# The attention's last four gated rows by seven products in front of w_o

## The chip, the cores and the metric

The kernel runs on one core of a Trainium2 chip. The metric is the device time of one execution in microseconds (us); lower is better. Before the change it is 2486.24 us, the median of three runs (2486.18 to 2487.11). The five engines named below are TensorE (PE, matrix products), VectorE (DVE), ScalarE (ACT), GpSimd (POOL) and SyncE (SP, which here issues the loads of weights). Each works through its own instructions in order and waits on semaphores for the others.

## The reference, cut to what matters

Two layers, each with a half-step feed-forward block, a mixer and another half-step feed-forward block. 640 tokens (512 of a new stream, 8 x 16 of running ones) share the weights; the model width is 1024. The change is inside the mixer:

```python
z = h @ w_in                                  # conv B | C | V | q | k | v | gates
g_conv, g_attn = split(sigmoid(g + b_gate))   # 1024 columns each
y_conv, _ = short_conv(B, C, V)               # 512 columns
y_attn = band_attention(q, k, v)              # 512 columns
m = g_conv * (y_conv @ w_conv_out) + g_attn * (y_attn @ w_attn_out)
x = x + m @ w_o
```

## The kernel before

Activations lie transposed: 128 features on the partitions, 640 tokens (T) along the free axis, in two halves of 320 (HT; `t1` and `t2`). Every float32 product is made of three matmuls of rounded parts, hi x hi, hi x lo and lo x hi; the parts of each weight and each operand are made on the chip, hi by an ACT cast and lo by a DVE subtraction. A plain product (`product`, line 434) of an output block of 128 features with 512 input features takes 4 x 3 x 2 = 24 matmuls of 128x128 by 320 columns.

Where it can, the kernel uses a seven-product scheme of the Strassen-Winograd kind in place of eight block products. Its seven operands are named X11, X21, X22, XT5 (parts of the input as it is, or one difference) and XN6, XT7, XT4 (mixtures of the two token halves of an even and an odd feature block). The weights are mixed too: a unit of kind "mix" is two raw tiles ra and rb, from which `source` (line 295 by way of `add`) makes four slabs: slab 0 is ra; slab 1 is a sum s and a sum in rb; slab 2 is a half that POOL has summed by an accumulating DMA (`one`, lines 280 and 281) and the half "raw<-s" that DVE sums; slab 3 is the second half of rb. A "plain" unit is one raw tile of eight 128x128 blocks. `prep` issues ACT's casts (whi, line 363), `flush` DVE's subtractions (wlo, line 368); slabs are prepared two ahead, with three buffers of each of raw, whi and wlo.

The mixer's second half is `outputs` (from line 1485 on). It runs with a written-out order: PE, DVE and ACT execute their instructions in the order of the program. It uses these pieces:

- `gate_pair(m)`: two gate columns m and m + 1 by seven products of 12 matmuls. PE works through X11, X21, XN6, XT5, XT7, X22, XT4. X11, XN6, XT7 and XT4 accumulate in one bank (pa, shown as qa). Between them ACT copies pa away: c1 after X11 (line 1512), u2 after XN6 (line 1522); c5 is copied out of pc after XT5 (line 1524). Between c1 and u2 ACT also has `due()` (sigmoids and copies that were put off), the casts of slab 2, what the hook at[0] does, and the cast of slab 3. DVE's add raw<-s for slab 2 is issued in the `prep` behind c1.
- `out(m)`: a plain product py of one output block (line 434), multiplied by its gate (line 1562), and, for the attention, added to the convolution's mm (line 295).
- `rows(name, ms)`: four output blocks at once by seven (line 1633), 84 matmuls, with their gating on DVE (lines 1640 and 1642). Before, only the convolution's blocks 4 to 7 go this way. `moved(0)` and `moved(1)` copy their gated results from the gates' buffers to mm by ACT (line 1647), moved(0) inside `rows`, ahead of its last product, and moved(1) in the `due` of the next pair.
- `mixed`: the DVE mixtures and parts of one pair of feature blocks of the convolution's y (lines 1590 and 1581), spread over the hooks.
- `take(ya)`: the parts of the attention's y (lines 234 and 235), in pair 8.
- `give(ms)`: the parts of the final m, spread over the last pair and the two last products; then w_o's eight products po (line 434), each over k = 0 to 7 in order, with x += po (line 1430) and the next block's operands (`ex.final`) behind each.

The gates' tiles take four rotating buffers; the banks of py, po and of the rows' two pairs of products take two; the parts of m take the eight buffers of the mixer's input h, which the gate pairs read to the end.

## Time and profile before

| what | value |
|---|---|
| median of 3 runs | 2486.24 us |
| profiled execution, its own time | 2487.08 us |
| its span, first to last instruction | 2485.3 us |
| mean granted TensorE clock | 0.999 |
| the mixer's second half, layer 0 / layer 1, seen from pair 8 to the end of w_o | 698.7 to 833.5 / 1930.1 to 2064.8 us |
| HBM read and written over the span | 99 GB/s |

Times in the profile are us from the span's start unless marked ns. A line in order of time gives the start, the duration, the engine, the line of the program, the operation with its output and inputs, the shapes, how many were merged, and in brackets how long the engine had idled and what released it. A matmul's own duration (0.31 us) is longer than its place in the pipeline, so the distance of starts counts.

### The profile page before, as it was taken

Reading aid. Unit: us, or ns where it says so; the run is one execution under the profiler, and the core shown is the slowest. Engines: PE = TensorE matmul, PEld = TensorE weight load, DVE = VectorE, ACT = ScalarE, POOL = GpSimd, SP = SyncE. Lnnn points to the kernel's source line nnn. Section 1 sums busy time; section 2 is a strip of 40 time slices with the busy share of each in tenths; the row PEclk is TensorE's granted clock in tenths of the full one; section 3 lists DMA queues with packets and bytes.
Section 4 is the critical chain, followed back from the end, with each engine's and each line's share of the span. In section 5 each row is a group of like instructions: output and inputs, shape, how many; then the busy total and the mean of one; then the engine's idle time right before and its main releaser. Section 6 shows DMA issues by size and latency. Waiting matters only on the chain.

```text
span 2485.3 us, 43991 instructions
## 1 busy us (share of the span) xinstructions
PE 2471.0 (99%) x17288; PEld 2418.2 (97%) x17288; DVE 2158.3 (87%) x3587; ACT 1373.0 (55%) x2196; POOL 317.4 (13%) x479
## 2 busy tenths in 40 slices
PE   9999999999999999999999999999999999999999
PEld 8999999889999999999999999998999999999998
DVE  7999998888886899998799999988878769999997
ACT  6555556665554555555665555556645455555555
POOL 0111112211000001111001111121110000111111
PEclk9999999999999999999999999999999999999999
DMA  4443445335343334444334443453453333443444
GB/s 155 126 118 102 123 119 121 113 109 177 104 118 108 94 101 106 112 117 120 108 94 109 110 118 102 116 128 107 132 173 92 115 111 89 107 116 106 113 117 117
DMA packets 113072, 287.11 MB, mean 116 GB/s; under 512 B 12928, under 2 KB 52480, under 8 KB 112864
## 3 DMA queue, kind: packets, MB, share of 16 engines
q1 hardware_dynamic: 69552, 220.10, 28.0%
q0 software_dynamic: 42880, 63.94, 13.7%
q8 instruction: 135, 2.21, 0.4%
q14 instruction: 73, 0.60, 0.1%
q10 hardware_dynamic: 432, 0.25, 0.0%
HBM read 238.43 MB, written 7.94 MB: 99 GB/s over the span
## 4 chain that ended last, share of the span: by engine, by line
PE 92%; DVE 4%; ACT 2%; DMA 1%; issue 1%; SPq 0%; DVEq 0%; ACTq 0%; POOLq 0%
PE pab L458 12%; PE paa L458 11%; PE pcb L458 6%; PE daa L1143 6%; PE pca L458 5%; PE dab L1143 5%; PE po L434 5%; PE qa L458 4%; PE py L434 3%; PE pbb L458 3%; PE dca L1143 3%; PE pba L458 3%; PE dcb L1143 2%; PE ma_qk L458 2%; PE ma_cv L458 2%; PE pv L1770 2%
## 5 line engine op out<-in xcount | busy, mean ns | idle before, releaser
L363 ACT CAST whi<-raw 128x512 fp32r<-128x512 f32 (+1 forms) x573 | 500.4, 878 | 371.3 <-PE pbb L458 46.0
L368 DVE TENSOR_TENSOR wlo<-raw,whi 128x512 fp32r<-128x512 f32 (+1 forms) x573 | 574.4, 1005 | 135.9 <-ACT whi L363 132.1
L363 ACT CAST whi<-s 128x1024 fp32r<-128x1024 f32 (+1 forms) x160 | 151.6, 947 | 313.3 <-issue 111.4
L458 PE MATMUL pab<-xhib,whi 128*128 128x320 f32 x704 | 217.5, 309 | 0.0
L458 PE MATMUL pab<-xlob,whi 128*128 128x320 f32 x704 | 217.0, 308 | 0.0
L458 PE MATMUL pab<-xhib,wlo 128*128 128x320 f32 x704 | 217.0, 308 | 0.0
L458 PE MATMUL paa<-xhia,whi 128*128 128x320 f32 x640 | 197.7, 309 | 0.2 <-DVE ga L295 0.2
L458 PE MATMUL paa<-xhia,wlo 128*128 128x320 f32 x640 | 197.5, 309 | 0.0
L458 PE MATMUL paa<-xloa,whi 128*128 128x320 f32 x640 | 197.4, 308 | 0.0
L368 DVE TENSOR_TENSOR wlo<-s,whi 128x1024 fp32r<-128x1024 f32 (+1 forms) x160 | 174.8, 1092 | 4.6 <-ACT whi L363 4.6
L1165 POOL DMA_DIRECT2D x<-c_a x80 | 70.0, 1022 | 573.8 <-ACT ahia L1047 205.5
L1165 POOL DMA_DIRECT2D x<-c_b x72 | 62.8, 1002 | 583.6 <-ACT ahib L1047 205.8
L458 PEld LDWEIGHTS pab<-xhib,whi 128*128 128x128 f32 x704 | 132.1, 188 | 0.9 <-issue 0.9
L458 PEld LDWEIGHTS pab<-xlob,whi 128*128 128x128 f32 x704 | 132.2, 188 | 0.0
L458 PEld LDWEIGHTS pab<-xhib,wlo 128*128 128x128 f32 x704 | 132.1, 188 | 0.0
L458 PEld LDWEIGHTS paa<-xhia,whi 128*128 128x128 f32 x640 | 120.1, 188 | 1.1 <-DVE ga L295 0.5
L458 PEld LDWEIGHTS paa<-xloa,whi 128*128 128x128 f32 x640 | 120.1, 188 | 0.2 <-DVE xloa L702 0.2
L458 PEld LDWEIGHTS paa<-xhia,wlo 128*128 128x128 f32 x640 | 120.1, 188 | 0.2
L295 DVE TENSOR_TENSOR raw<-s,raw 128x512 f32<-128x512 f32 x160 | 109.1, 682 | 0.0
L458 PE MATMUL pcb<-xhib,wlo 128*128 128x320 f32 x352 | 108.7, 309 | 0.0
L458 PE MATMUL pcb<-xlob,whi 128*128 128x320 f32 x352 | 108.5, 308 | 0.0
L458 PE MATMUL pcb<-xhib,whi 128*128 128x320 f32 x352 | 108.5, 308 | 0.0
(840 smaller groups left out, 8150.4 us busy)
## 6 DMA issues: line engine op xcount, KB each, us to landing
raw<-in_wst SPq DMA_DIRECT2D x375, 512.0 KB, 3.6
x<-c_a POOLq DMA_DIRECT2D x80, 160.0 KB, 4.6
x<-c_b POOLq DMA_DIRECT2D x72, 160.0 KB, 3.6
lent<-in_wst POOLq DMA_DIRECT2D x36, 256.0 KB, 3.9
kc<-in_kcache SPq DMA_DIRECT2D x32, 256.0 KB, 5.2
vc<-in_vcache SPq DMA_DIRECT2D x16, 512.0 KB, 4.8
one<-in_wst POOLq DMA_DIRECT2D x28, 256.0 KB, 4.1
x<-u_a POOLq DMA_DIRECT2D x40, 160.0 KB, 4.1
```

The costliest lines, as they stand in the source:

```text
L295: DVE.tensor_tensor(out=out, in0=a, in1=b, op=op)
L363: ACT.copy(hi[:, d], src[:, c])
L368: DVE.tensor_tensor(out=lo, in0=src, in1=hi.bitcast(F32), op=ALU.subtract)
L434: PE.matmul(ps[:, a, :HT], w, x[a] if isinstance(x, tuple) else x[:, a * HT : (a + 1) * HT], start=first and j == 0 and not seeded, stop=l ...
L458: PE.matmul(ps, a, b, start=start and kp == 0 and j == 0, stop=stop and kp == NP - 1 and j == 2, skip_group_check=True)
L1143: PE.matmul(ps[u], w, y, start=start and i == 0 and j == 0, stop=i == 1 and j == 2, skip_group_check=True)
L1165: POOL.dma_start(x[ms[2 * u + r]][:, cols], z[:, u], accum_op=ALU.add)
L1770: PE.matmul(pv[t], xx[:, t * P : (t + 1) * P], w[:, kk * AW : (kk + 1) * AW], start=c == 0 and kk == 0 and j == 0, stop=c == KT // 2 - 1 a ...
```

## The change

The attention's blocks 4 to 7 leave `out` and go through `rows`, so that they need the mixtures of the attention's y as well. The order becomes: pair 8, py 8 and 9, pair 10, py 10 and 11, pair 12, pair 14, rows. The mixtures of both pairs of feature blocks are made in one instruction each: `mix(0)` to `mix(3)` on DVE behind py 8 and py 9, their hi parts (`high`) on ACT and lo parts (`rest`) on DVE in the hooks of pairs 10 and 12 and behind py 10. The operand tiles of the two pairs become one tile of two. moved(0) goes from the convolution's rows into the `due` of pair 8, moved(1) into its at[0], and the gates' buffers are taken behind that `due`. The parts of m are made in another order: m 0 and 2 in pair 14, 1 and 3 inside the rows, 4 to 7 behind them. w_o's two first products are interleaved: k = 0, 2, 1, 3 of both, then k = 4 to 7 of both.

```diff
     out += gates[:2] + [("co", m) for m in range(4)] + gates[2:4] + [("rows", ("co", (4, 5, 6, 7)))]
-    for i in range(4):
+    for i in range(2):
         out += [gates[4 + i], ("ao", 2 * i), ("ao", 2 * i + 1)]
+    out += gates[6:] + [("rows", ("ao", (4, 5, 6, 7)))]
     return out + [("o", m) for m in range(KT)]
...
             hold[0] = True
+            first = [acc(f"po{l}_{m}") for m in range(2)]
+            ws = [[tiles.take() for _ in mo] for _ in first]
+            for ks in ((0, 2, 1, 3), range(KT // 2, KT)):
+                for p, w in zip(first, ws):
+                    for k in ks:
+                        multiply(p, w[k], mo[k], k == 0, k == KT - 1)
             for m in range(KT):
-                po = acc(f"po{l}_{m}")
-                product(po, mo)
+                po = first[m] if m < 2 else acc(f"po{l}_{m}")
+                if m > 1:
+                    product(po, mo)
                 ex.weights(m)
...
-            u, g = gates[m], gates[m + 1] = tmp(f"g{n}"), tmp(f"g{n}_1")
             s0 = quiet()
             block(pa, s0, 0, X11, every, True, True)
             ACT.copy(c1, pa)
             due()
+            u, g = gates[m], gates[m + 1] = tmp(f"g{n}"), tmp(f"g{n}_1")
             prep(used[0] + 1)
...
+        def minus(out, a):
+            DVE.scalar_tensor_tensor(out=out, in0=a, scalar=-1.0, in1=out, op0=ALU.mult, op1=ALU.subtract)
...
+        za = yas.rearrange("p (i c) (a b) -> p i (c a) b", i=2, a=2)
+
+        def mix(n):
+
+            e1, e2, o1, o2 = (za[:, :, k] for k in range(4))
+            if n == 0:
+                add(e1, e1, e2, ALU.subtract)
+            elif n == 1:
+                add(e2, o2, e2, ALU.subtract)
+            else:
+                minus(*((o2, e1) if n == 2 else (o1, o2)))
+
+        def place(k):
+            if k == XT5:
+                return [(*(u[:, t2] for u in ya[2 * i]), za[:, i, 0]) for i in range(2)]
+            c = EXTRA.index(k)
+            return [(*(u[:, :, c] for u in x["ao"]), za[:, :, 1 + c])]
+
+        def high(*ks):
+            for k in ks:
+                for hi, _, z in place(k):
+                    ACT.copy(hi, z)
+
+        def rest(*ks):
+            for k in ks:
+                for hi, lo, z in place(k):
+                    low(lo, z, hi)
...
             gated(0, [s1[:, u] for u in range(2)], t1)
+            if mid:
+                mid()
             mul(c, w, 1, XT5, True)
...
             gated(0, [s2[:, u] for u in range(2)], t2)
-            if then:
-                then()
-            if name == "co":
-                moved(0)
             mul(a, w, 0, XT4, False)
-            flush()
+            if not end:
+                flush()
             gated(1, a, t1, -1.0)
             if name == "co":
-                lates.append(lambda: moved(1))
+                lates.append(lambda: moved(0))
+                moves.append(lambda: moved(1))
+            if end:
+                flush()
...
+        def begun(*ms):
+            for m in ms:
+                mo[m] = tuple(hp.tile([P, T], F32R, tag=f"h{i}", name=f"m{l}_{m}{i}") for i in ("hi", "lo"))
+
+        def given(*ms):
+            for m in ms:
+                split(*mo[m], mm[m])
...
-        rows("co", (4, 5, 6, 7), yc)
-        for m in range(KT, 2 * KT, 2):
-            last = m == 2 * KT - 2
-            gate_pair(m, [none, none, (lambda: take(ya, "ya", range(CT), yas_)) if m == KT else
-                          (lambda: give(range(1))) if last else none])
-            out(m, ya, (lambda: give(range(1, 4))) if last else None)
-            out(m + 1, ya, (lambda: give(range(4, 6))) if last else None)
-        give(range(6, KT))
+        rows("co", (4, 5, 6, 7), None)
+        gate_pair(8, [lambda: moves[0](), none, lambda: take(ya, "ya", range(CT), srcs)])
+        room("ao")
+        out(8, ya, None, lambda: (mix(0), mix(1)))
+        out(9, ya, None, lambda: (mix(2), mix(3)))
+        gate_pair(10, [lambda: high(XN6), lambda: (rest(XN6), high(XT7)), lambda: (rest(XT7), high(XT4))])
+        out(10, ya, None, lambda: rest(XT4))
+        out(11, ya)
+        gate_pair(12, [lambda: high(XT5), lambda: rest(XT5), none])
+        gate_pair(14, [none, lambda: (begun(*range(4)), given(0, 2)), none])
+        rows("ao", (4, 5, 6, 7), None, lambda: given(1, 3), None, True)
+        begun(*range(4, KT))
+        total(4, 5)
+        given(4)
+        total(6, 7)
+        given(5, 6, 7)
         return mo
```

The host lays out the weight stream by the same order (`mixer_order`): four plain slabs of w_attn_out become two plain ones and a unit of kind mix, so that the number of raw tiles stays the same. `total(ms)` adds the gated rows to mm (before, `out` did so for all eight blocks), and `room("ao")` takes the shared tile of the mixtures' parts.

More of the change, by code (lines that the diff above doesn't have):

```diff
@@ L1566, in out @@
                 post()
-        yc, ya, mo = [], [], []
-        more = []
-        yas_ = [yas[:, c, :] for c in range(CT)]
+        yc, ya = [], []
+        mo = [None] * KT
+        srcs = [yas[:, c, :] for c in range(CT)]
+        x, moves = {}, []
         def take(y, name, cs, srcs):
@@ L1574, in take, with take_even, room, mixed @@
                 y.append(parts(gp, f"y{c}", f"{name}{l}_{c}", srcs[c]))
-        def give(ms):
-            for m in ms:
-                mo.append(parts(hp, "h", f"m{l}_{m}", mm[m]))
+        def take_even(c):
+            y = tuple(gp.tile([P, T], F32R, tag=f"y{c}{i}", name=f"ya{l}_{c}{i}") for i in ("hi", "lo"))
+            split(*(z[:, t1] for z in y), srcs[c][:, t1])
+            ya.append(y)
         def low(lo, z, hi):
             DVE.tensor_tensor(out=lo, in0=z, in1=hi.bitcast(F32), op=ALU.subtract)
-        def mixed(i, y, z):
-            z = z.rearrange("p c (a b) -> p (c a) b", a=2)
-            e1, e2, o1, o2 = (z[:, i] for i in range(4))
+        def room(name):
+            x[name] = tuple(gp.tile([P, 2, 3, HT], F32R, tag=f"x{i}", name=f"x{i}{name}{l}") for i in ("hi", "lo"))
+        def minus(out, a):
+            DVE.scalar_tensor_tensor(out=out, in0=a, scalar=-1.0, in1=out, op0=ALU.mult, op1=ALU.subtract)
+        def mixed(i):
+            z = ycp[i].rearrange("p c (a b) -> p (c a) b", a=2)
+            e1, e2, o1, o2 = (z[:, k] for k in range(4))
             add(e1, e1, e2, ALU.subtract)
             add(e2, o2, e2, ALU.subtract)
-            for out, a in ((o2, e1), (o1, o2)):
-                DVE.scalar_tensor_tensor(out=out, in0=a, scalar=-1.0, in1=out, op0=ALU.mult, op1=ALU.subtract)
+            minus(o2, e1)
+            minus(o1, o2)
             yield
-            hi, lo = (gp.tile([P, 3, HT], F32R, tag=f"x{i}{p}", name=f"x{p}{l}_{len(more)}") for p in ("hi", "lo"))
+            hi, lo = (u[:, i] for u in x["co"])
             ACT.copy(hi, z[:, 1:])
-            more.append((hi, lo))
             yield
@@ L1597, in mixed @@
             yield
-            hi, lo = (u[:, t2] for u in y[2 * i])
+            hi, lo = (u[:, t2] for u in yc[2 * i])
             ACT.copy(hi, e1)
@@ L1602, in mixed, with kind, rows @@
             yield
-        def take_even(c, src):
-            y = tuple(gp.tile([P, T], F32R, tag=f"y{c}{i}", name=f"ya{l}_{c}{i}") for i in ("hi", "lo"))
-            split(*(z[:, t1] for z in y), src[:, t1])
-            ya.append(y)
+        za = yas.rearrange("p (i c) (a b) -> p i (c a) b", i=2, a=2)
[20 more added lines that the diff above has]
+                    low(lo, z, hi)
         EXTRA = XT7, XT4, XN6
-        def kind(y, i, k):
+        def kind(name, i, k):
             if k in EXTRA:
-                return tuple(z[:, EXTRA.index(k)] for z in more[i - 2])
-            hi, lo = y[2 * i + (k in (X21, X22))]
+                return tuple(z[:, i, EXTRA.index(k)] for z in x[name])
+            hi, lo = (yc if name == "co" else ya)[2 * i + (k in (X21, X22))]
             return tuple(z[:, t2 if k in (X22, XT5) else t1] for z in (hi, lo))
-        def rows(name, ms, y, then=None):
+        def rows(name, ms, first, mid=None, late=None, end=False):
             n = f"{name}{l}_{ms[0]}"
@@ L1630, in mul @@
                         wh, wl = (z[:, kp * P : (kp + 1) * P] for z in s)
-                        xh, xl = kind(y, i, k)
+                        xh, xl = kind(name, i, k)
                         for j, (w, x_) in enumerate(((wh, xh), (wh, xl), (wl, xh))):
@@ L1654, in rows @@
             flush()
+            if first:
+                first()
             mul(b, w, 1, X21, True)
@@ L1670, in rows @@
             gated(1, [s5[:, u] for u in range(2)], t2, -1.0)
+            if late:
+                late()
             mul(c, w, 1, X22, False)
@@ L1675, in rows @@
             gated(0, [s2[:, u] for u in range(2)], t2)
-            if then:
-                then()
-            if name == "co":
-                moved(0)
             mul(a, w, 0, XT4, False)
-            flush()
+            if not end:
+                flush()
             gated(1, a, t1, -1.0)
             if name == "co":
-                lates.append(lambda: moved(1))
-        def total(m0, m1):
-            for m in range(m0, m1):
-                add(mm[m], mm[m], gates[KT + m])
+                lates.append(lambda: moved(0))
+                moves.append(lambda: moved(1))
@@ L1690, in outputs, with total, going @@
+            if end:
+                flush()
+        def total(*ms):
+            for m in ms:
+                add(mm[m], mm[m], gates[KT + m])
+        def begun(*ms):
+            for m in ms:
+                mo[m] = tuple(hp.tile([P, T], F32R, tag=f"h{i}", name=f"m{l}_{m}{i}") for i in ("hi", "lo"))
+        def given(*ms):
+            for m in ms:
+                split(*mo[m], mm[m])
         none = lambda: None
-        def also(*fs):
-            return lambda: [f() for f in fs]
-        def going(z):
-            return lambda: next(z)
+        def going(*zs):
+            return lambda: [next(z) for z in zs]
@@ L1698, in outputs @@
         gate_pair(2, [none, none, lambda: take(yc, "yc", range(CT), ycs)])
-        z = [mixed(i, yc, ycp[i]) for i in range(2)]
+        z = [mixed(i) for i in range(2)]
+        room("co")
         out(0, yc, None, going(z[0]))
-        out(1, yc, None, also(going(z[0]), going(z[1])))
-        out(2, yc, None, also(going(z[0]), going(z[1])))
+        out(1, yc, None, going(*z))
+        out(2, yc, None, going(*z))
         out(3, yc, None, going(z[1]))
-        both = also(going(z[0]), going(z[1]))
@@ L1705, in outputs @@
-        gate_pair(4, [both, both, none])
+        gate_pair(4, [going(*z), going(*z), none])
         gate_pair(6, [none] * 3)
-        rows("co", (4, 5, 6, 7), yc)
-        for m in range(KT, 2 * KT, 2):
-            last = m == 2 * KT - 2
-            gate_pair(m, [none, none, (lambda: take(ya, "ya", range(CT), yas_)) if m == KT else
-                          (lambda: give(range(1))) if last else none])
-            out(m, ya, (lambda: give(range(1, 4))) if last else None)
-            out(m + 1, ya, (lambda: give(range(4, 6))) if last else None)
```

## The prediction

> **What bounds the kernel now.** I read the profile page first, then the table of stretches around the edited code, then PE's, ACT's and DVE's instructions in order of time in the first layer, and held the second layer against it.

> ```profile
> span 2485.3 us, 43991 instructions
> PE 2471.0 (99%) x17288; PEld 2418.2 (97%) x17288; DVE 2158.3 (87%) x3587; ACT 1373.0 (55%) x2196; POOL 317.4 (13%) x479
> ```

> PE sets the time: it is busy for 2471.0 of 2485.3 us and leads nearly all of the chain that ended last. A matmul taken away counts in full, and so does a stall put in.

> ```profile
> 698.70:718.50 19.80, 19.68 (x134) 19.36 (x133) 17.50 (x31) 13.51 (x22) 1.44 (x2) 1.00 0.46 119
> ```

> This is the stretch of gate pair 8 with the products py 8 and 9 in layer 0 (columns: length, busy PE, weight loads, DVE, ACT, POOL, clock, DMA). The same stretch of layer 1 has the same counts and, to a few hundredths, the same times, so I work out one layer and double it. DVE is busy for 17.50 of 19.80 us there: it has little room, and this is where the change puts its new DVE work.

> **The matmuls saved.** Rows 4 to 7 of the attention were four products of 24 matmuls, 96 in all; by seven they are 7 x 12 = 84.

> ```profile
> 711.62 7.04 PE py L434 x48
> ```

> 48 matmuls of 320 columns take 7.04 us, 146.7 ns each. Twelve fewer are **-1.76 us** a layer. [...]

> **The first gate pair after the convolution's rows (pair 8).** Here the change moves four ACT copies, moved(0) and moved(1).

> ```profile
> 698.72 0.31 PE L458 MATMUL qa<-hhim,whi 128*128 128x320 f32 x1
> ...
> 702.09 0.31 PE L458 MATMUL qb<-hhim,wlo 128*128 128x320 f32 x1
> 702.52 0.41 PE L458 MATMUL qa<-thi,whi 128*128 128x320 f32 x1
> ...
> 706.14 0.36 PE L458 MATMUL qa<-thi,whi 128*128 128x320 f32 x1
> ...
> 718.50 0.31 PE L458 MATMUL qa<-hhim,whi 128*128 128x320 f32 x1
> ...
> 725.53 0.31 PE L458 MATMUL qa<-thi,whi 128*128 128x320 f32 x1
> ```

> ```profile
> 700.79 1.35 ACT L1647 COPY yc<-g 128x640 f32<-128x640 f32 x2 [0.78 <-DVE g L1640]
> 702.05 0.41 ACT L1512 COPY capsm<-qa 128x320 f32<-128x320 f32 x1
> 702.80 1.36 ACT L1647 COPY yc<-g 128x640 f32<-128x640 f32 x2 [0.33 <-DVE g L1642]
> 704.06 0.62 ACT L363 CAST whi<-one 128x512 fp32r<-128x512 f32 x1
> 704.58 1.14 ACT L363 CAST whi<-raw 128x512 fp32r<-128x512 f32 x2
> 705.62 0.41 ACT L1522 COPY capsm<-qa 128x320 f32<-128x320 f32 x1
> 707.61 0.72 ACT L234 CAST ya_0hi<-ya 128x640 fp32r<-128x640 f32 x1
> 708.24 0.73 ACT L234 CAST ya_1hi<-ya 128x640 fp32r<-128x640 f32 x1
> ...
> 722.46 1.15 ACT L363 CAST whi<-raw 128x512 fp32r<-128x512 f32 x2 [1.05 <-DVE raw L295]
> 723.98 0.43 ACT L1522 COPY capsm<-qa 128x320 f32<-128x320 f32 x1 [0.38 <-PE qa L458]
> ```

> PE may not accumulate XN6 into bank qa before ACT has copied c1 out of it, nor XT7 before ACT has copied u2. Today c1 stands behind moved(0) (702.05 + 0.41 = 702.46), and XN6 begins at 702.52, 0.28 late; with 0.10 more at its restart and 0.05 before 706.14 I count 0.43 lost. After, c1 is copied on time and XN6 isn't late. But moved(0) then runs from 701.2 (its DVE input, below, ends there) to 702.5, whi<-one to 703.0, and the next cast must wait for DVE's raw<-s, which ends at 703.08 + 0.68 = 703.76. Behind that come a cast (0.52), moved(1) (1.26), a cast (0.52) and u2 (0.41): 703.82 + 2.71 = 706.53. PE would be ready for XT7 at 698.72 + 7.04 = 705.76, so it stops for 0.83, with a restart of 0.10 for 0.93. Net **+0.50**. Bounds 0 (moved(1) runs in the gap) and +0.6.

> **The second gate pair (pair 10), behind the mixtures.** mix(0) to mix(3) stand on DVE behind py 8 and py 9, ahead of the add raw<-s that pair 10 needs.

> ```profile
> 654.53 1.01 DVE L295 TENSOR_TENSOR yc<-yc 128x320 f32<-128x320 f32 x2
> ...
> 656.51 0.82 DVE L1560 TENSOR_TENSOR mm<-py,g 128x640 f32<-128x640 f32 x1
> ...
> 683.16 0.49 DVE L295 TENSOR_TENSOR g<-qa,c 128x320 f32<-128x320 f32 x1 [2.39 <-PE qa L458]
> ...
> 695.47 0.82 DVE L295 TENSOR_TENSOR rs<-raco,rs 128x640 f32<-128x640 f32 x1 [0.96 <-PE raco L1633]
> ...
> 697.34 0.69 DVE L295 TENSOR_TENSOR raw<-raw 128x512 f32<-128x512 f32 x1
> ...
> 698.67 0.89 DVE L1642 SCALAR_TENSOR_TENSOR g<-rs,g 128x320 f32<-128x320 f32 x2
> ...
> 700.28 0.88 DVE L1640 TENSOR_TENSOR g<-rs,g 128x320 f32<-128x320 f32 x2
> 701.08 0.68 DVE L368 TENSOR_TENSOR wlo<-s,whi 128x512 fp32r<-128x512 f32 x1
> ...
> 702.28 0.88 DVE L1642 SCALAR_TENSOR_TENSOR g<-raco,g 128x320 f32<-128x320 f32 x2
> 703.08 0.68 DVE L295 TENSOR_TENSOR raw<-s,raw 128x512 f32<-128x512 f32 x1
> ...
> 709.15 1.22 DVE L368 TENSOR_TENSOR wlo<-raw,whi 128x1024 fp32r<-128x1024 f32 x1
> ...
> 718.20 0.83 DVE L295 TENSOR_TENSOR mm<-mm,g 128x640 f32<-128x640 f32 x1
> 718.94 0.68 DVE L368 TENSOR_TENSOR wlo<-s,whi 128x512 fp32r<-128x512 f32 x1
> ...
> 721.74 0.69 DVE L295 TENSOR_TENSOR raw<-s,raw 128x512 f32<-128x512 f32 x1
> ```

> A 640-wide DVE operation takes its place for 0.74 us (718.20 to 718.94); four are 2.96 at least. Two pairs mixed one by one, as the convolution does it, take 2 x 1.98 = 3.96 (654.53 to 656.51): the upper bound. Two dependent ones of 320 columns take 1.01 together (654.53) where two independent ones take 0.88 (700.28), so I add 0.13 for each of two dependences: 3.2. [...]

> DVE has no gap in this stretch that could take the 3.2. I stay on the present clock of pair 10, which begins at 718.50 and wants XT7 at 725.53. raw<-s moves from 721.74 to 724.94 and ends at 725.63. ACT's cast of raw waits for it (today: 1.05 us idle until that same add), and runs to 726.2; high(XN6), a 640-wide cast, takes 0.63 (707.61 to 708.24) to 726.8; the cast of the last slab 0.52 to 727.3; then u2, 0.43, to 727.75. PE is held for 2.25, and with a restart of 0.10 this is **+2.35**. With the bounds of the mixtures it is 2.1 to 3.1; below that only if ACT need not wait (first rival). The weights themselves are on time: wlo<-one follows raw<-s directly. Once PE has been held for 2.35, DVE and ACT have that much more time before pair 12, and it hides rest(XT4), high(XT5) and rest(XT5): 0 for them; without that cover each would cost at most its own 0.74.

> **Into w_o.**

> ```profile
> 776.23 0.46 PE L434 MATMUL py<-ya_3hi,wlo 128*128 128x320 f32 x2
> 776.75 0.53 PE L434 MATMUL po<-m_0hi,whi 128*128 128x320 f32 x2
> 777.12 0.45 PE L434 MATMUL po<-m_0lo,whi 128*128 128x320 f32 x2
> ...
> 782.10 0.46 PE L434 MATMUL po<-m_6hi,whi 128*128 128x320 f32 x2
> 782.46 0.56 PE L434 MATMUL po<-m_6lo,whi 128*128 128x320 f32 x2
> 782.86 0.45 PE L434 MATMUL po<-m_6hi,wlo 128*128 128x320 f32 x2
> ```

> Two matmuls take 0.29, so 0.23 + 0.08 is lost on entry and 0.07 + 0.11 at m_6: 0.49, which the new order drops (**-0.49**). What DVE has to do instead: in the convolution's rows its last gating ends 4.4 us behind PE (703.1 against 698.72). In the attention's rows the parts of m_1 and m_3 (1.48, less the 0.96 idle, with 0.1 of lag) add 0.6, the sums for a following mixture (697.34 to 698.67) take 1.3 away, and the two weight splits (701.08 to 702.28) 1.2, as only plain slabs follow: 2.5 behind. Then come a 1.2 split of a plain slab (709.15), four adds and four splits of 0.74: m_4 is done 5.9 and m_7 9.6 us after PE's last matmul of the rows. PE spends 7.04 on the first half of two products, so it wants m_4 at 7.3 and m_7 at 10.0. It fits by 0.4. I take **+0.20** for small waits here and in the rows; bounds 0 and 1.0. The parts of m_0 and m_2 lie in the 2.39 us that DVE idles in a pair between pairs (683.16, pair 6, as pair 14 will be) and the rest of w_o is the same work. Moved DMAs: the weight stream keeps its count of slabs, only the order within it changes, and one more POOL load (one) runs a pair ahead; 0, hidden by the buffer that is filled a pair early.

> **Sum.** -1.76 + 0.50 + 2.35 - 0.49 + 0.20 = +0.80 a layer, +1.6 for two. The profiled execution took 2487.08 us, 1.8 more than its span; that gives 2488.7. The median was 0.84 below it, so the forecast is **2487.8 us**, own range, by the bounds of the terms, 2485.9 (-0.15 a layer) to 2491.1 (+2.45 a layer).

> **Rivals.** (a) ACT isn't held in pair 10, because the mixtures cost DVE little or u2 gets ahead: the sum without 2.35 is -1.55 a layer, **2483.1 us**. For it: the convolution has the same order (mixture parts ahead of u2) and loses nothing. Against it: there the add starts early enough; here DVE comes 3.2 us later. (b) No new wait at all: -1.76 - 0.43 - 0.49 = -2.68 a layer, **2480.9**. Against it: moved(1) visibly stands between two casts and u2. (c) DVE becomes the bound at w_o's entry: if it is 2 us further behind than I reckon, m_7 comes 1.6 us late, and as m_5 to m_7 come one by one nothing hides it; from 0.4 us of extra lag on, each us costs one. With 2.2 us more, +1.8 a layer, it gives **2491.4**. For it: DVE is full in these rows. Against it: pair 14 lets it catch up. (d) w_o's new order doesn't remove the entry stall: +0.49 a layer, **2488.8**.

> **Chances.** Forecast 0.58, (a) 0.17, (b) 0.06, (c) 0.12, (d) 0.07. The range that leaves out (b) and most of (c) is 2482.5 to 2491.0. What this measurement can tell from no change is about 0.2%, 5 us: 2481.3 to 2491.2. Faster than that is (b), 0.06; slower is (c), 0.12; the rest, 0.82, is the same.

> **What would show it.** In the changed profile: a stop of PE of about 2 us at pair 10's XT7, released by ACT's copy of capsm from qa, with ACT idle on DVE's raw before it; about 0.8 at pair 8's XT7 and none at its XN6; 84 matmuls where 96 were; no gap at po's first matmul. The forecast is wrong if ACT's cast in pair 10 isn't late, or if po waits for more than a us on m_4 to m_7.

## The result, and the profile after

The changed kernel takes 2492.61 us (median of 12 runs, 2489.84 to 2493.68), the kernel before 2486.41 us (12 runs, 2486.18 to 2487.11). The ratio is 1.0023, 95% interval 1.0014 to 1.0031: slower, by 6.2 us between the medians, and 1.6 above 2491.0, the top of the forecast range. The spread has grown as well, from 0.9 to 3.8 us. The profiled execution took 2493.24 us. One of 31 executions of the kernel before (3439.64 us, granted clock 0.65) and one of 11 of the kernel with all three edits (2991.43 us, 0.75) were in a slower state and are left out of the medians below.

The page of the changed kernel, first lines:

```profile
span 2491.5 us, 44039 instructions
PE 2471.4 (99%) x17264; PEld 2418.2 (97%) x17264; DVE 2183.1 (88%) x3635; ACT 1385.1 (56%) x2222; POOL 320.2 (13%) x483
```

24 matmuls are gone, 12 a layer as forecast, but busy PE has not become less (2471.0 before): the matmuls that are left took longer somewhere. DVE has gained 24.8 us of work.

From the start of pair 8 to the end of w_o, layer 0 took 698.72 to 833.47 before and takes 698.78 to 836.78 now: +3.25 us. Layer 1 has the same stops at the same places and gains the same 3.25. The two make 6.5; the rest of the program gave 0.3 back. PE's instructions in order of time show the stops of layer 0 (line numbers are one to some sixty higher than before):

```profile
706.62 0.42 PE L459 MATMUL qa<-thi,whi 128*128 128x320 f32 x1 [0.65 <-ACT capsm L1530]
...
728.34 0.64 PE L459 MATMUL qa<-thi,whi 128*128 128x320 f32 x1 [2.10 <-ACT capsm L1530]
728.77 0.47 PE L459 MATMUL qa<-tlo,whi 128*128 128x320 f32 x1
...
779.27 0.46 PE L435 MATMUL po<-m_0hi,whi 128*128 128x320 f32 x2
...
788.42 0.41 PE L435 MATMUL po<-m_5lo,whi 128*128 128x320 f32 x1 [0.77 <-DVE m_5lo L236]
```

The bracket counts from the modelled end of the last matmul. A stop "by the starts" is the distance of two starts less the usual 0.147. By the starts, PE is 0.82 late at pair 8's XT7, 2.26 late at pair 10's XT7, not late at po's first matmul, and 0.94 late at m_5's low part. The first two are released by ACT's copy u2 (capsm). ACT and DVE ahead of the second one, in order of time:

```profile
720.69 1.68 DVE L296 TENSOR_TENSOR ya<-ya 128x640 f32<-128x640 f32 x2
722.29 0.82 DVE L1570 TENSOR_TENSOR g<-py,g 128x640 f32<-128x640 f32 x1
723.14 0.83 DVE L296 TENSOR_TENSOR mm<-mm,g 128x640 f32<-128x640 f32 x1
723.88 1.68 DVE L1597 SCALAR_TENSOR_TENSOR ya<-ya 128x640 f32<-128x640 f32 x2
725.48 0.69 DVE L296 TENSOR_TENSOR raw<-s,raw 128x512 f32<-128x512 f32 x1
```

```profile
726.20 0.62 ACT L364 CAST whi<-raw 128x512 fp32r<-128x512 f32 x1 [4.25 <-DVE raw L296]
726.72 0.72 ACT L1640 CAST xhiao<-ya 128x640 fp32r<-128x640 f32 x1
727.35 0.61 ACT L364 CAST whi<-raw 128x512 fp32r<-128x512 f32 x1
727.87 0.42 ACT L1530 COPY capsm<-qa 128x320 f32<-128x320 f32 x1
```

The mixtures take 720.69 to 722.29 and 723.88 to 725.48, 3.2 us. ACT idles 4.25 us for raw<-s, then casts raw, the mixture and the last slab before it can copy u2, and PE goes on 0.05 after that copy ends.

What I hadn't forecast comes after it. The table of stretches (length, busy PE, weight loads, DVE, ACT, POOL, granted clock, DMA share, GB/s):

```profile
726.00:728.30 2.30, 0.24 (x2) 0.00 (x0) 2.16 (x5) 2.10 (x5) 0.57 (x1) 1.00 0.01 4
728.30:729.00 0.70, 0.66 (x2) 0.66 (x3) 0.70 (x2) 0.70 (x2) 0.00 (x0) 0.54 0.74 234
...
730.00:731.00 1.00, 1.00 (x6) 1.00 (x5) 0.00 (x0) 0.81 (x2) 0.63 (x1) 0.50 0.86 336
731.00:732.00 1.00, 1.00 (x6) 1.00 (x5) 0.00 (x0) 0.00 (x0) 0.23 (x1) 0.62 0.91 342
732.00:733.00 1.00, 1.00 (x9) 1.00 (x8) 0.96 (x3) 0.00 (x0) 0.00 (x0) 1.00 1.02 240
```

For 3.41 us behind the stop the clock granted to PE is half ("half clock" below), and 12 to 13 matmuls come 0.27 us apart instead of 0.147: about 1.5 us lost. In layer 1 the clock falls 1.5 us after PE has gone on again, for as long.

At w_o's entry, DVE in order of time:

```profile
781.59 1.22 DVE L369 TENSOR_TENSOR wlo<-raw,whi 128x1024 fp32r<-128x1024 f32 x1
782.72 1.56 DVE L296 TENSOR_TENSOR yc<-yc,g 128x640 f32<-128x640 f32 x2
784.19 1.23 DVE L369 TENSOR_TENSOR wlo<-raw,whi 128x1024 fp32r<-128x1024 f32 x1
785.33 0.83 DVE L236 TENSOR_TENSOR m_4lo<-yc,m_4hi 128x640 fp32r<-128x640 f32 x1
786.06 1.56 DVE L296 TENSOR_TENSOR yc<-yc,g 128x640 f32<-128x640 f32 x2
787.53 0.83 DVE L236 TENSOR_TENSOR m_5lo<-yc,m_5hi 128x640 fp32r<-128x640 f32 x1
```

The split at 784.19 belongs to w_o's third weight slab, which PE doesn't want for another 9 us. In the program's text it stands behind all parts of m; here it runs ahead of m_4's. Two blocks with a written-out order follow each other there, and the order between the blocks isn't written out; the first experiment tests whether that is the cause.

So the theory for the experiments is: per layer -1.76 (matmuls), +0.50 (pair 8), +2.36 (pair 10), +1.5 (half clock behind that stop), -0.49 (old entry waits), +1.04 (m_5, by the slab's split that ran ahead) = +3.15, against 3.25 measured.

### The profile page after: what moved, and what is told of

It is laid out like the page before. It is cut to its first block, busy times and chain, and to the rows that moved or that the text cites. A ratio compares the mean times of both kernels' runs of the same rounds, so it can differ in the third digit from the quotient of the medians.

```text
span 2491.5 us, 44039 instructions
## 1 busy us (share of the span) xinstructions
PE 2471.4 (99%) x17264; PEld 2418.2 (97%) x17264; DVE 2183.1 (88%) x3635; ACT 1385.1 (56%) x2222; POOL 320.2 (13%) x483
## 4 chain that ended last, share of the span: by engine, by line
PE 89%; DVE 6%; ACT 2%; issue 2%; DMA 1%; SPq 0%; DVEq 0%; ACTq 0%; POOLq 0%
PE pab L459 12%; PE paa L459 11%; PE pcb L459 6%; PE daa L1144 6%; PE pca L459 5%; PE dab L1144 5%; PE po L435 4%; PE qa L459 3%; PE pbb L459 3%; PE dca L1144 3%; PE pba L459 3%; PE dcb L1144 2%; PE ma_cv L459 2%; PE pv L1827 2%; PE ma_qk L459 2%; PE py L435 2%
```

## The experiments

Four edits came first, beside runs of the kernel before on the same chip (2486.83 us).

**The order at w_o's entry.** w_o's two first products move into the block of the parts of m:

```diff
                 mo = outputs(l, gp, ops.X, st, cs, ycp, yas, sigmoid, gates)
+                first = [acc(f"po{l}_{m}") for m in range(2)]
+                ws = [[tiles.take() for _ in mo] for _ in first]
+                for ks in ((0, 2, 1, 3), range(KT // 2, KT)):
...
         ex = after()
         with tc.manual_schedule(engines=ORDERED):
             hold[0] = True
-            first = [acc(f"po{l}_{m}") for m in range(2)]
...
```

> The changed kernel with one thing undone: w_o's first two products are issued inside the same written-out order as the parts of m, so that the split of w_o's third weight slab can't run ahead of m_4's. Theory (that split, 1.14 us, makes m_5 late): the wait of 0.94 us at m_5 goes, about 1.0 us a layer, 2.1 us in all: 2490.5 against 2492.6 where the clock behaves the same. Rival (DVE simply has more work in the rows than I reckoned): no change, the wait at m_5 stays near 0.9.

Measured: 2489.50 us (2488.55 to 2491.44). DVE in order of time:

```profile
780.30 1.22 DVE L369 TENSOR_TENSOR wlo<-raw,whi 128x1024 fp32r<-128x1024 f32 x1
781.44 1.55 DVE L296 TENSOR_TENSOR yc<-yc,g 128x640 f32<-128x640 f32 x2
783.05 0.82 DVE L236 TENSOR_TENSOR m_4lo<-yc,m_4hi 128x640 fp32r<-128x640 f32 x1
783.79 1.55 DVE L296 TENSOR_TENSOR yc<-yc,g 128x640 f32<-128x640 f32 x2
785.26 0.82 DVE L236 TENSOR_TENSOR m_5lo<-yc,m_5hi 128x640 fp32r<-128x640 f32 x1
...
787.47 1.22 DVE L369 TENSOR_TENSOR wlo<-raw,whi 128x1024 fp32r<-128x1024 f32 x1
```

```profile
786.20 0.49 PE L435 MATMUL po<-m_5lo,whi 128*128 128x320 f32 x2
```

The split now runs at 787.47, behind m_7, m_5 comes in time, and the 0.94 us of wait is gone from PE in both layers (at most 0.07 is left). The order was the cause, not the amount of DVE's work. From po's first matmul to the end of w_o the profiles give 57.35 us for the changed kernel and 56.36 here, 1.0 less as expected. The median fell by 3.1 instead of 2.1, at least in part because the clock fell less often: in the profiled execution it didn't fall at all, the four executions with a mean granted clock of 1.000 took 2488.55 to 2489.34, and the two with 0.998 took 2490.79 and 2491.44.

**The mixtures behind u2.**

```diff
-        out(8, ya, None, lambda: (mix(0), mix(1)))
-        out(9, ya, None, lambda: (mix(2), mix(3)))
-        gate_pair(10, [lambda: high(XN6), lambda: (rest(XN6), high(XT7)), lambda: (rest(XT7), high(XT4))])
-        out(10, ya, None, lambda: rest(XT4))
-        out(11, ya)
-        gate_pair(12, [lambda: high(XT5), lambda: rest(XT5), none])
-        gate_pair(14, [none, lambda: (begun(*range(4)), given(0, 2)), none])
+        out(8, ya)
+        out(9, ya)
+        gate_pair(10, [none, lambda: (mix(0), mix(1), mix(2)), none])
+        out(10, ya, None, lambda: (mix(3), high(XN6)))
+        out(11, ya, None, lambda: high(XT7, XT4))
+        gate_pair(12, [none, lambda: (rest(XN6, XT7, XT4), high(XT5)), none])
+        gate_pair(14, [lambda: rest(XT5), lambda: (begun(*range(4)), given(0, 2)), none])
```

> The changed kernel with the mixtures moved behind u2 of pair 10 and to py 10 and 11, their parts to pairs 12 and 14. Theory (the stop of 2.26 us comes from the mixtures ahead of raw<-s, and the half clock behind it comes from the stop): both go, 2.36 + 1.45 a layer, 7.6 us: about 2485.0, and a spread between runs as small as before the change. Rival (the clock falls for another reason, such as the denser work of the new order): only the stop goes, 4.7 us: 2487.9, with matmuls at half clock left somewhere in these stretches.

Measured: 2485.40 us (2485.10 to 2486.14). The stop of pair 10 is gone, no matmul of these stretches runs at half clock, and the spread is down to 1.0 us. The stops of pair 8 (0.82) and of m_5 are still there:

```profile
784.48 0.56 PE L435 MATMUL po<-m_5lo,whi 128*128 128x320 f32 x2 [0.79 <-DVE m_5lo L236]
```

The half clock went together with the stop, while the denser order of the new rows stayed: that speaks against the rival.

**A shorter stop.** Only high(XN6) goes behind u2:

```diff
-        gate_pair(10, [lambda: high(XN6), lambda: (rest(XN6), high(XT7)), lambda: (rest(XT7), high(XT4))])
+        gate_pair(10, [none, lambda: (high(XN6), rest(XN6), high(XT7)), lambda: (rest(XT7), high(XT4))])
```

> The changed kernel with only the cast high(XN6) moved behind u2 in pair 10. Theory: the stop shrinks by that cast, from 2.26 to 1.63 us, 1.3 us in two layers. If the clock falls after any stop of this kind, the 1.45 us a layer stay: 2491.3. If a stop must be longer than some 2 us for it, they go too: 2488.4. Rival (ACT isn't what holds PE): no change, 2492.6.

Measured: 2489.17 us (2488.52 to 2490.30).

```profile
727.89 0.41 PE L459 MATMUL qa<-thi,whi 128*128 128x320 f32 x1 [1.48 <-ACT capsm L1530]
728.15 0.31 PE L459 MATMUL qa<-tlo,whi 128*128 128x320 f32 x1
728.29 0.31 PE L459 MATMUL qa<-thi,wlo 128*128 128x320 f32 x1
```

The stop is 1.64 us by the starts, and the matmuls behind it come 0.14 apart at once. The time is 0.8 above the 2488.4 expected without a fall of the clock and 2.1 below the 2491.3 with one.

**The stop without the change.** The kernel before, with five idle subtractions on DVE behind py 8 and py 9; they overwrite the attention's y where nothing reads it any more:

```diff
+            spare = lambda n: [low(yas_[i % 4], yas_[i % 4], yas_[(i + 1) % 4]) for i in range(n)] if m == KT else None
-            out(m, ya, (lambda: give(range(1, 4))) if last else None)
-            out(m + 1, ya, (lambda: give(range(4, 6))) if last else None)
+            out(m, ya, (lambda: give(range(1, 4))) if last else None, lambda: spare(2))
+            out(m + 1, ya, (lambda: give(range(4, 6))) if last else None, lambda: spare(3))
```

> The kernel before with five idle subtractions of 640 columns on DVE behind py 8 and py 9 (they change the attention's y where nothing reads it any more). Theory: raw<-s comes 3.7 to 4.2 us later, u2 with it, and PE stops 2.2 to 2.7 us at XT7 of pair 10; the clock falls behind the stop in most runs and costs 1.45: about 3.8 to 4.2 a layer, 2486.4 + 8 = 2494 to 2495, and 2491.3 in runs whose clock doesn't fall. Rival (the half clock belongs to the new order, not to the stop): 2491.3 in all runs and a clock of 1.00 in the profile.

Measured: 2493.63 us (2491.48 to 2495.78).

```profile
728.07 0.42 PE L458 MATMUL qa<-thi,whi 128*128 128x320 f32 x1 [2.34 <-ACT capsm L1522]
728.33 0.31 PE L458 MATMUL qa<-tlo,whi 128*128 128x320 f32 x1
```

The stop of 2.50 us is there without any mixture or new row: DVE work ahead of raw<-s is enough. The profiled execution, 2491.48 us, is the fastest of nine and has no half clock; it agrees with the 2491.3 expected for that. The other eight lie 1.4 to 4.3 us above it. This run's profile shows no fall of the clock; that the others fell in one layer or in both is read from each execution's mean granted clock. A fall of 3.41 us to half takes 0.0007 from it, and the record rounds it to three places: 1.000 for the 2491.48, 0.999 for the four of 2492.90 to 2493.63, 0.998 for the four of 2494.92 to 2495.78. This fits none, one and two falls.

**More of the same.** The numbers of idle subtractions go from 2 and 3 to 4 and 5.

> The kernel before with nine idle subtractions on DVE instead of five. The stop at XT7 of pair 10 grows by 4 x 0.8 = 3.2 to about 5.7 us. If the half clock lasts a fixed time behind a stop, it costs 1.4 to 1.7 in every run: 2486.4 + 2 x (5.7 + 0.1 + 1.6) = 2501. If its cost grows with the stop, 2503 or more. If the stop has nothing to do with it, 2498.

Measured: 2502.92 us (2502.11 to 2503.79; before on that chip 2486.52).

```profile
731.35 0.63 PE L458 MATMUL qa<-thi,whi 128*128 128x320 f32 x1 [5.76 <-ACT capsm L1522]
731.78 0.47 PE L458 MATMUL qa<-tlo,whi 128*128 128x320 f32 x1
```

```profile
731.40:737.40 6.00, 6.00 (x23) 6.00 (x24) 2.90 (x5) 1.18 (x2) 0.86 (x1) 0.50 0.77 235
1970.70:1976.40 5.70, 5.70 (x22) 5.70 (x23) 2.82 (x5) 1.15 (x2) 0.86 (x1) 0.50 0.80 244
```

After a stop of 5.92 us the clock is half for the whole of the 6.0 and 5.7 us shown, in both layers, and all four executions lie within 1.7 us. So the fall is caused by the stop, and its cost can grow with it: some 22 matmuls, 2.7 us, against 1.5 behind 2.26 us. It grows in a step: by the record of the clock it is half for 6.83 us here, twice the 3.41 of before, and PE stands for the first 0.8 to 1.0 of them. This is nearer to the growing cost (2503 or more) than to the fixed one (2501).

The next four ran side by side on one chip (before: 2486.41 us).

**moved(1) behind the parts of y.**

```diff
-        gate_pair(8, [lambda: moves[0](), none, lambda: take(ya, "ya", range(CT), srcs)])
+        gate_pair(8, [none, none, lambda: (take(ya, "ya", range(CT), srcs), moves[0]())])
```

> The changed kernel with moved(1) alone put elsewhere: out of at[0] of pair 8 and behind the parts of the attention's y, late in the same pair. Theory: u2 of pair 8 comes at about 705.3 where XT7 wants it at 705.8, the stop of 0.82 + 0.11 goes: 1.9 us in two layers against the changed kernel on the same chip. Rival (moved(0), or the add raw<-s itself, is what holds u2): less than 0.5 us.

Measured: 2490.89 us (2488.14 to 2492.36), the changed kernel beside it 2491.66 (below). PE and ACT around pair 8's XT7:

```profile
705.66 0.31 PE L459 MATMUL qc<-hhim,wlo 128*128 128x320 f32 x1
705.81 0.31 PE L459 MATMUL qa<-thi,whi 128*128 128x320 f32 x1
```

```profile
703.86 1.14 ACT L364 CAST whi<-raw 128x512 fp32r<-128x512 f32 x2 [0.92 <-DVE raw L296]
704.91 0.42 ACT L1530 COPY capsm<-qa 128x320 f32<-128x320 f32 x1
```

The stop is gone: XT7 follows XT5 without a gap. The medians differ by 0.8 us only and don't settle the size, as the falls of the clock are larger than it. The profiles do: from pair 8 to po's first matmul a layer takes 79.56 us here and 80.49 in the first profile of the changed kernel, and in both of them the clock falls in both layers. The 0.93 between them is the 0.82 + 0.11 expected.

**All three edits together.**

> The changed kernel with all three edits: w_o's first two products in the same written-out order as the parts of m, the mixtures behind u2, moved(1) behind the parts of y. If the three waits are all that the change put in, what is left is the sum of its gains, 1.76 + 0.43 + 0.49 = 2.7 a layer: 2486.8 - 5.3 = 2481.5. Rival (a wait removed comes back elsewhere, as DVE is full): 2483 or more.

Measured: 2481.83 us (ratio 0.9981, interval 0.9972 to 0.9991). Run again on another chip:

> The kernel with all three edits once more, for a profile at full clock and a narrower interval: 2481.4 to 2482.8, 4.4 us less than before the change. Theory: no stop over 0.2 us between pair 8 and the end of w_o. Rival: one of the three waits is left over in part, as the median is 0.5 above the sum of the gains.

Measured: 2481.88 us against 2486.52; ratio 0.9982, interval 0.9973 to 0.9991. ACT at pair 10, in order of time:

```profile
722.67 1.14 ACT L364 CAST whi<-raw 128x512 fp32r<-128x512 f32 x2 [1.06 <-DVE raw L296]
724.18 0.43 ACT L1530 COPY capsm<-qa 128x320 f32<-128x320 f32 x1 [0.37 <-PE qa L459]
```

u2 now waits for PE and not PE for u2, and nothing between pair 8 and the end of w_o is late by more than 0.07 us. This kernel is 4.6 us faster than the one before and, on the same chip, 9.8 faster than the changed one (2491.66): the three waits, with the half clock behind one of them, are what took the gain. 0.6 us of the 5.3 expected are missing between the medians. The profiles show 5.1 of the 5.3 in the two stretches from pair 8 to the end of w_o (132.03 us a layer instead of 134.58); where the rest is stays open.

**Without w_o's split.** The edits of the mixtures and of moved(1), and w_o's products in the plain order:

```diff
-            first = [acc(f"po{l}_{m}") for m in range(2)]
...
-                po = first[m] if m < 2 else acc(f"po{l}_{m}")
-                if m > 1:
-                    product(po, mo)
+                po = acc(f"po{l}_{m}")
+                product(po, mo)
```

> The changed kernel with the mixtures behind u2, moved(1) behind the parts of y, and w_o's products in the plain order of before (k = 0 to 7 of the first, then of the second), parts of m as changed. PE then wants m_4 3.8 us behind the rows and m_7 at 6.5; DVE has them at 6.9 and 10.6. Theory (DVE's parts are the bound there): a stop of some 4 us in all at w_o's entry per layer, spread over m_4 to m_7, about 2483.5 + 6 to 8 = 2490 to 2492, more if the clock falls. Rival (the split of the two products is worth little): within 1 us of 2483.5.

Measured: 2492.53 us (2489.05 to 2493.44).

```profile
779.75 0.56 PE L435 MATMUL po<-m_4hi,whi 128*128 128x320 f32 x2 [1.41 <-ACT m_4hi L235]
780.61 0.56 PE L435 MATMUL po<-m_4lo,whi 128*128 128x320 f32 x2 [0.30 <-DVE m_4lo L236]
...
782.82 0.42 PE L435 MATMUL po<-m_5lo,whi 128*128 128x320 f32 x1 [1.06 <-DVE m_5lo L236]
```

By the starts PE waits 1.57, 0.47 and 1.23 us, 3.3 in all, in each layer, and the clock falls behind these, for 3.41 us in layer 0 and 6.83 in layer 1. From po's first matmul to the end of w_o the layers take 61.41 and 62.66 us, 5.0 and 6.3 more than with all three edits. Without the two interleaved products the attention's rows by seven don't pay in this order: the split is worth more than the rows' matmuls, 1.76 a layer.

**The changed kernel again**, beside those:

> The changed kernel once more, on the same chip as the three beside it, so that they can be set against it: 2490 to 2493.7 as before, by how often the clock falls.

Measured: 2491.66 us (2490.13 to 2493.83). The profiled execution has the stop of 2.26 us in both layers, but the half clock behind it in layer 0 alone; two stretches, behind the stop of layer 0 and around the end of that of layer 1:

```profile
728.60:732.00 3.40, 3.40 (x15) 3.40 (x15) 1.03 (x3) 2.18 (x3) 0.86 (x1) 0.50 0.80 290
1960.81:1964.20 3.39, 1.87 (x12) 1.87 (x13) 2.52 (x4) 3.39 (x7) 0.57 (x1) 1.00 0.52 172
```

From pair 8 to po's first matmul, layer 0 takes 80.48 us and layer 1 78.95. In the kernel before, the two layers take 78.03 and 78.04. So the same instructions in one execution differ by the fall alone, and its price is 1.53 us.

## Why the prediction was wrong, point by point

- **The matmuls:** right. 24 are gone, and with the waits removed as well the kernel gains 4.6 us of the 5.3 expected.
- **Pair 8:** right in place, cause and size: 0.83 and 0.10 forecast, 0.82 and 0.11 measured, and no wait at XN6. Moving moved(1) removes it.
- **Pair 10:** the stop itself was right in place, cause and size: 2.25 forecast, 2.26 measured, by mixtures of 3.2 us as reckoned. Moving the mixtures removes it.
- **What follows the stop:** this is the first step that failed. The sum ended at "PE is held for 2.25, and with a restart of 0.10 this is +2.35"; it took for granted that PE runs on at the speed of before. It ran on at half clock, +1.5 a layer in the profiled execution. No rival had it. The trace of before has no stop over 0.83 us between PE's first and last matmul, so it couldn't show that 2.26 are enough; but its first matmuls, from 5.60 to 10.9 us, come 0.267 us apart and those behind them 0.147, so that it did show PE starting at little more than half its later rate. What a stop does to the clock was first shown by the runs behind the prediction: in their profiles half clock lasts 3.41 us in each layer with the 2.26 of the changed kernel and 6.83 with the 5.92 of the nine idle subtractions, and there is none with the 1.64 of the shorter stop.
- **Into w_o:** the second step that failed. The old waits went as forecast (0.49). But "Then come a 1.2 split of a plain slab (709.15), four adds and four splits" left out a second split, which in the program's text stands behind them. DVE's own work was reckoned rightly: with that split in its place (the first experiment) m_4 is done 5.9 us and m_7 9.6 us behind the rows, as forecast; in the changed kernel it is 6.9 and 10.6. The small-waits term was sized +0.20 and measured 1.04, just over its upper bound of 1.0. Rival (c) had the place and the price ("from 0.4 us of extra lag on, each us costs one"), though not the cause.
- **The sum:** +0.80 a layer forecast, +3.25 measured; of the 2.45 between them the half clock is 1.5 and the entry 0.84.
- **The chances:** 0.82 on the same within 0.2%, and the result is 0.23% slower. Either of the two terms, put right, would have left the median inside the range (2492.6 less 3.0 or less 1.7); it took both to leave it.

## What to carry to other kernels

Where one engine sets the time, an operation moved to a "free" engine is priced by the first instruction behind it in that engine's queue that the bounding engine waits for: here four DVE operations (3.2 us) and a cast (0.63 us) stood ahead of one 0.43 us copy out of a bank, and PE stopped for 2.26 us. Put such work behind the copy, where the same engines idle waiting for PE (with all three edits ACT waits 1.33 us for it next, and the stop is gone). And a stop of TensorE like these 2.26 us isn't priced by its length alone: add the half clock that may follow it, 1.5 us a layer in this kernel, in some executions and not in others.

## What the runs showed of the hardware

| stop of PE by the starts | longest part of it in one window | what followed |
|---|---|---|
| 0.82 us (pair 8, changed kernel) | 0.82; 0.64 us | full clock, both layers |
| 1.64 us (high behind u2) | 1.56; 1.65 | full clock, both layers |
| 2.26 us (w_o's order mended) | 1.52; 1.33 | full clock, both layers |
| 2.50 us (five idle subtractions) | 1.71; 1.65 | full clock, both layers |
| 2.26 us (changed kernel again) | 2.26; 1.53 | half clock for one window in layer 0, full clock in layer 1 |
| 2.26 us (changed kernel) | 2.26; 1.87 | half clock for one window, both layers |
| 2.26 us (moved(1) behind the parts of y) | 2.06; 2.26 | half clock for one window, both layers |
| 5.92 us (nine idle subtractions) | 3.41; 3.41 | half clock for two windows, both layers |

In this table the fall doesn't go with the length of the stop (2.50 us without it, 2.26 with it) but with how much of one window PE stood still: up to 1.72 us of a window (the first part of the stop of 5.92) left the clock full, 1.87 and more were followed by half clock in the next window. By it the same stop of 2.26 us halved the clock in some executions and not in others (1.33 to 1.53 of it in one window without a fall, 1.87 to 2.26 with one), and the fall in layer 1 of the changed kernel began 1.5 us after PE had gone on again, at the window's end. Nothing between 1.72 and 1.87 was measured, and the three short stops without w_o's split, with 1.70 us of standing still and three restarts in one window, were followed by half clock as well. In these runs the clock came back after a window in which PE worked throughout; one with a stop of 0.6 to 1.0 us in it kept it at half (nine idle subtractions, and layer 1 without w_o's split).

The falls account for a good part of the scatter: 3.8 us for the changed kernel, 1.0 with the mixtures behind u2. Not for all of it: the executions with all three edits scatter over 1.5 and 2.9 us, with no stop left in the profile.
